# Two up tiles of a gated feed-forward from seven quarter products instead of eight

## The chip, the cores and the metric

The kernel runs on one core of one Trainium2 chip. The metric is the device time of one execution, in microseconds (us). The time of the kernel before is the median of three executions. Fractions of a microsecond per repetition matter here, because the part that is changed is repeated twenty times.

The engines are named as the profile names them: PE is the matrix engine, PEld its weight loads (they overlap PE), DVE the vector engine, ACT the scalar engine, POOL the general-purpose one, and SP the queue that issues the transfers (DMAs). Each engine works its own instructions in order, and engines wait for each other by semaphores.

## The reference, cut to what matters

The model is a two-layer decoder trunk on 512 tokens of width 1024. Only the feed-forward block of each layer matters for the change:

```python
def rms_norm(x, g):
    y = x * lax.rsqrt(jnp.mean(x * x, axis=-1, keepdims=True) + EPS)
    return y * g

def swiglu(h, w_gate_up, w_down):                  # D_FF = 2816 = 22 tiles of 128
    gu = h @ w_gate_up
    return (silu(gu[..., :D_FF]) * gu[..., D_FF:]) @ w_down

for layer in range(2):
    x = x + concat([mix_out, mem_o]) @ w_out[layer]
    x = x + swiglu(rms_norm(x, ln_ffn[layer]), w_gate_up[layer], w_down[layer])
return rms_norm(x, ln_final)
```

The norm is `x * gain * rstd`, where `rstd` is one number for each token. The kernel projects `x * gain` and multiplies by `rstd` afterwards. Each of the gate and the up half has 22 tiles of 128 rows.

## The kernel before, in words

**Layout.** Everything is kept transposed: features on the 128 partitions, the 512 tokens (T) along the row. The width of 1024 (D) is eight tiles of 128 (KD = 8). A weight tile is `[128, 1024]`: for one tile of 128 outputs, its eight blocks of 128x128 lie side by side, block k for input tile k.

**Precision.** Every operand of a projection is split into a rounded part and a rest, `hi` and `lo` (`split`, `weight`, `pair`). ACT writes `hi` (`copy`, L137), DVE writes `lo = src - hi` (`tt`, L150). `mm3` issues three matmuls (L143): hi by hi, hi by lo, lo by hi. One projection of 1024 by 512 tokens (`project`) is 8 blocks times 3 = 24 matmuls of 512 columns, accumulated in one PSUM bank.

**Weights.** `load` starts the transfer of a raw tile into one of two buffers `wraw` (512 KB each); `weight` splits it into `whi` and `wlo`, three buffers each, used in turn. So a new split can be written when the matmuls of the projection three before it have read theirs, and a new transfer can start when the `lo` of the tile two before it is done.

**Feed-forward (`ffn`).** Two halves of 11 tiles. For each tile f of a half: project gate (PSUM tag `pj`) and up (tag `g`); DVE multiplies the gate by `rstd` into `fg`; ACT applies silu; POOL multiplies `fg` by `rstd` again; DVE multiplies it with the up result into `fu`, and `fu` is split into the pair that the down projection reads. Then the down projection: for each of 8 output tiles 33 matmuls over 11 blocks, and DVE adds the sum to `x[m]`. In layer 0 the rotary tables (`rope_tables`, some 20 DVE instructions and two sines) are written beside the first gate tiles. In layer 1 the last two down tiles are done in two halves of 256 tokens, with the final norm behind each (`final`, `store`).

**Order.** The program is written as if sequential; a scheduler then puts the instructions of each engine in order and adds the semaphores. That order is fixed before the run. The `output` stage (w_out) lies ahead of each feed-forward; it produces `x[m]`, the pairs `h[m]`, and the sum of squares behind `rstd`.

Of the kernel before, what the change touches and what calls it, by code (L numbers as in the profile page):

```python
# [9 lines left out]
F32 = mybir.dt.float32  # L10
# [8 lines left out]
P = 128  # L19
# [66 lines left out]
class Builder:  # L86
# [52 lines left out]
    def square(self, out, in_):  # L139
        return self.nc.scalar.activation(out, in_, AF.Square).ins  # L140

    def mm(self, out, lhsT, rhs, start=True, stop=True):
        return self.nc.tensor.matmul(out, lhsT, rhs, start=start, stop=stop).ins  # L143

    def tr(self, out, in_):
        k = in_.shape[0]
# [29 lines left out]
        self.nc.sync.dma_start(raw, src)  # L176
        return raw

    def weight(self, src, eng=None, raw=None, parts=1, pool=None):

        raw = self.load(src) if raw is None else raw
        n = raw.shape[1]
        hi = self.t(pool or self.wpool, [P, D], F32R, "whi", 3)[:, :n]
        lo = self.t(pool or self.wpool, [P, D], F32R, "wlo", 3)[:, :n]
        for i in range(parts):
            s = slice(i * n // parts, (i + 1) * n // parts)
            self.split(raw[:, s], hi[:, s], lo[:, s], eng or self.weng)
        return hi, lo

    def mm3(self, ps, w, k, act, start, stop):  # L190

        (wh, wl), (ah, al) = w, act
        s = slice(k * P, (k + 1) * P)
        self.mm(ps, wh[:, s], ah, start, False)
        self.mm(ps, wh[:, s], al, False, False)
        self.mm(ps, wl[:, s], ah, False, stop)

    def project(self, src, acts, tag="pj", order=range(KD), w=None):
        w = self.weight(src) if w is None else w
# [26 lines left out]
    def build(self):  # L226
        tc, nc, a = self.tc, self.nc, self.a
        with ExitStack() as st:
            opened = lambda name, **kw: tc.tile_pool(name=name, bufs=1, reuse_waits="tile", **kw)
            pool = lambda name, **kw: st.enter_context(opened(name, **kw))  # L230
            cp = pool("const")
            self.wpool, self.apool = pool("w"), pool("acta")
            self.dpool = pool("scratch", space=DRAM)
            self.load_constants(cp)
            self.weng = nc.vector
            with opened("layer0", side="right") as self.mpool:
                with self.banks(pj=3, g=2, sc=3):
                    with opened("early", side="right") as ep:
                        self.mem_and_norm(ep)
                        self.gates(ep)  # L240
                    with opened("gdn", side="right") as gp:
                        mix = self.gdn(gp)
                    self.bpool, xp = pool("actb"), pool("x")
                    self.x = [self.t(xp, [P, T], F32, f"x{k}") for k in range(KD)]
                    for k in range(KD):
                        nc.sync.dma_start(self.x[k], a["xT"][:, k, :])
                    self.rstd, self.cosT, self.sinT = (self.t(xp, [P, T], F32, n) for n in ("rstd", "cosT", "sinT"))
                    h = self.output(xp, 0, mix, self.bpool)
                with opened("ffn0", side="right") as fp, self.banks(pj=4, g=4):
                    self.ffn(fp, xp, 0, h, self.apool, rope=True)  # L250
            with self.banks(pj=2, g=1, qk=1, pt=2, sc=1):
                with opened("swa", side="right") as sp:
                    mix = self.swa(sp)
                h = self.output(xp, 1, mix, self.apool)
            with opened("ffn1", side="right") as fp, self.banks(pj=4, g=4):
                self.ffn(fp, xp, 1, h, self.bpool)
# [570 lines left out]
        return h  # L827

    def ffn(self, fp, xp, layer, h, apool, rope=False):
        nc, a = self.nc, self.a  # L830
        acc = self.acc
        half = FT // 2
        for f0 in (0, half):
            acts = []
            for f in range(f0, f0 + half):
                pg = self.project(a["wgu"][layer, 2 * f], h, "pj")
                pu = self.project(a["wgu"][layer, 2 * f + 1], h, "g")
                if f == 0:
                    self.rstd_from(acc)
                    self.use(SILU_SIN)  # L840
                g = self.t(fp, [P, T], F32, "fg", 2)
                self.tt(nc.vector, g, pg, self.rstd, ALU.mult)
                self.fn(g, g, AF.Silu)
                self.tt(nc.gpsimd, g, g, self.rstd, ALU.mult)
                u = self.t(fp, [P, T], F32, "fu", 2)
                self.tt(nc.vector, u, pu, g, ALU.mult)
                hl = self.pair(apool) if f - f0 < KD else self.pair(fp, f"ac{f - f0}")
                self.split(u, *hl)
                acts.append(hl)
                if rope and f == 4:  # L850
                    self.rope_tables(fp)
            self.acc = None
            tail = KD - 2 if f0 and layer else KD
            down = lambda m, j, n, **kw: self.weight(a["wdn"][layer, m][:, (f0 + j) * P:(f0 + j + n) * P], **kw)
            for m in range(tail):
                ps = self.bank("pj")
                for j, n in ((0, 6), (6, 5)):
                    w = down(m, j, n)
                    for k in range(n):
                        self.mm3(ps, w, k, acts[j + k], j + k == 0, j + k == half - 1)  # L860
                self.tt(nc.vector, self.x[m], ps, self.x[m], ALU.add)
                if f0:
                    self.acc = self.accumulate(xp, self.acc, self.x[m], m)
        if tail < KD:

            parts = (slice(0, T // 2), slice(T // 2, T))
            w = {m: [down(m, j, n, pool=fp if m == KD - 1 else None) for j, n in ((0, 6), (6, 5))] for m in range(tail, KD)}
            outs = [self.t(fp, [P, KD, t.stop - t.start], F32, f"fin{t.start}") for t in parts]
            for o, t in zip(outs, parts):
                for k in range(tail):  # L870
                    self.copy(o[:, k, :], self.x[k][:, t], scale=self.gain(G_FIN, k))
            ends = []
            for t in parts:
                acc = self.acc[:, t]
                for m in range(tail, KD):
                    ps = self.bank("pj")[:, t]
                    for k in range(half):
                        self.mm3(ps, w[m][k // 6], k % 6, [x[:, t] for x in acts[k]], k == 0, k == half - 1)
                    x = self.x[m][:, t]
                    self.tt(nc.vector, x, ps, x, ALU.add)  # L880
                    sq = self.t(fp, [P, T], F32, "sql", 2)[:, t]
                    self.square(sq, x)
                    if m < KD - 1:
                        nxt = self.t(fp, [P, T], F32, "sqb", 2)[:, t]
                        self.tt(nc.vector, nxt, acc, sq, ALU.add)
                        acc = nxt
                ends.append(self.final(fp, (acc, sq), t))
            for (ps, r), o, t in zip(ends, outs, parts):
                self.store(ps, r, o, t, tail)

    def rstd_from(self, acc, t=slice(0, T)):
        self.use(LN_EXP)
# [15 lines left out]
    def rope_tables(self, pool):  # L908
# [1 line left out]
        nc, a = self.nc, self.a  # L910
        pi = self.t(pool, [P, T], I32, "rpi")
        nc.sync.dma_start(pi, a["positions"].partition_broadcast(P))
        r = self.t(pool, [P, T], F32, "rr")
        n = self.t(pool, [P, T], F32, "rn")
        nc.vector.tensor_copy(r, pi)
        self.ts(r, r, self.consts[:, C_INV:C_INV + 1], ALU.mult)
        magic = 1.5 * 2.0 ** 23
# [6 lines left out]
        sn = self.t(pool, [P, T], F32, "rsn")  # L924
        self.fn(sn, r, AF.Sin)
        self.ts(self.sinT, sn, self.consts[:, C_SIGN:C_SIGN + 1], ALU.mult)

# [87 lines left out]
    def final(self, fp, squares, t):  # L1015
# [5 lines left out]
        l, r = (self.t(fp, [P, T], F32, n, 2)[:, t] for n in ("fl", "fr"))  # L1021
# [5 lines left out]
    def store(self, ps, r, o, t, done):  # L1027

        nc = self.nc
        rows = self.a["out"].rearrange("(k p) t -> p k t", p=P)  # L1030
        wide = lambda f, k: f.unsqueeze(1).to_broadcast([P, k, t.stop - t.start])
        send = lambda a, b: nc.sync.dma_start(rows[:, a:b, t], o[:, a:b, :])
        self.tt(nc.gpsimd, o[:, 0:2, :], o[:, 0:2, :], wide(r, 2), ALU.mult)
        for k in range(2, done, 2):
            self.tt(nc.vector, o[:, k:k + 2, :], o[:, k:k + 2, :], wide(ps, 2), ALU.mult)
            send(k, k + 2)
        for k in range(done, KD):
            self.stt(o[:, k, :], self.x[k][:, t], self.gain(G_FIN, k), ps, ALU.mult, ALU.mult)
        send(done, KD)
        send(0, 2)  # L1040


def layout(i):
# [56 lines left out]
```

## Time and profile before

| what | value |
|---|---|
| time, median of 3 | 1200.42 us (1200.05 to 1201.89) |
| the profiled execution's own time | 1200.59 us, with a span of 1198.8 us in the profile |
| PE busy | 1178.0 us (98%), 6042 matmuls |
| PEld busy | 962.2 us (80%) |
| DVE busy | 620.2 us (52%), 1056 instructions |
| ACT busy | 507.0 us (42%), 938 instructions |
| POOL busy | 92.3 us (8%), 61 instructions |
| granted TensorE clock | 0.998 |

The span goes from the first to the last instruction; the time has 1.8 us more around it. Matmuls are pipelined: a row of the profile gives one matmul from its issue to its modelled end, so the sum of the rows is more than PE's time, and what one costs in a stream is the distance from one start to the next. The name `out<-in` beside an instruction gives the tiles that it writes and reads.

### The profile page before, as it was taken

The page shows a single profiled execution, that of the slowest core. Times are in us where ns is not written, and L with a number is a line of the kernel's source. Part 1 is how long each engine was busy: PE and PEld are TensorE (multiplying, and loading weights), DVE is VectorE, ACT ScalarE, POOL GpSimd, SP SyncE. Part 2 cuts the span into 40 slices and gives each one's busy share as a digit, 9 for nine tenths or more (in the row PEclk, how much of TensorE's full clock was granted, in tenths as well). Part 3 has the DMA queues.
Part 4 walks back from the last instruction along what each step waited for, and adds up shares of the span by engine and source line. Part 5 has one row for each costly group of instructions (what it writes and reads, how often), then busy time and mean ns, then how long its engine had stood idle before and what let it go on. Part 6 is the DMA issues. An engine that isn't in the chain of part 4 may idle for free.

```text
span 1198.8 us, 15416 instructions
## 1 busy us (share of the span) xinstructions
PE 1178.0 (98%) x6042; PEld 962.2 (80%) x6042; DVE 620.2 (52%) x1056; ACT 507.0 (42%) x938; POOL 92.3 (8%) x61
## 2 busy tenths in 40 slices
PE   7999999999999999999999999999999999999997
PEld 6888777877888888888888876788888888888886
DVE  6654977767754433334434767764434333434343
ACT  7578672466432322232333546773323222323342
POOL 0310000000011110011110000000111100111100
PEclk9999999999999999999999999999999999999999
DMA  7424352324333223333323320113232233232232
GB/s 298 138 91 127 98 127 83 117 75 170 100 93 92 97 79 96 113 104 93 97 76 97 131 79 28 54 52 108 88 106 88 81 93 126 88 106 88 77 96 92
DMA packets 51037, 121.08 MB, mean 101 GB/s; under 512 B 14300, under 2 KB 17012, under 8 KB 50964
## 3 DMA queue, kind: packets, MB, share of 16 engines
q1 hardware_dynamic: 50964, 120.10, 31.9%
q8 instruction: 47, 0.77, 0.3%
q14 instruction: 26, 0.21, 0.1%
HBM read 113.12 MB, written 6.96 MB: 100 GB/s over the span
## 4 chain that ended last, share of the span: by engine, by line
PE 91%; DVE 5%; ACT 2%; DMA 1%; issue 0%; SPq 0%; DVEq 0%; ACTq 0%
PE pj L143 59%; PE g L143 24%; PE sc L143 6%; PE pt L147 1%; DVE wlo L150 1%; PE g L147 1%; ACT sm L131 1%; DMA wraw<-in_wmk 1%; DVE btmp L150 1%; DVE big L150 0%; DVE sm L739 0%; DMA big<-basein 0%; PE qk L143 0%; DVE q L150 0%; ACT whi L137 0%
## 5 line engine op out<-in xcount | busy, mean ns | idle before, releaser
L137 ACT ACTIVATE whi<-wraw 128x1024 fp32r<-128x1024 f32 (+2 forms) x213 | 207.6, 976 | 555.9 <-PE pj L143 348.0
L143 PE MATMUL pj<-h,whi 128*128 128x512 f32 (+1 forms) x980 | 382.7, 391 | 0.2
L143 PE MATMUL pj<-l,whi 128*128 128x512 f32 (+1 forms) x980 | 381.4, 389 | 0.0
L143 PE MATMUL pj<-h,wlo 128*128 128x512 f32 (+1 forms) x980 | 381.1, 389 | 0.0
L150 DVE TENSOR_TENSOR wlo<-wraw,whi 128x1024 fp32r<-128x1024 f32 (+2 forms) x213 | 238.4, 1119 | 143.8 <-ACT whi L137 143.3
L143 PEld LDWEIGHTS pj<-h,whi 128*128 128x128 f32 x980 | 184.0, 188 | 39.8 <-issue 3.1
L143 PEld LDWEIGHTS pj<-l,whi 128*128 128x128 f32 x980 | 184.2, 188 | 38.3 <-issue 2.0
L143 PEld LDWEIGHTS pj<-h,wlo 128*128 128x128 f32 x980 | 184.3, 188 | 38.0 <-issue 1.9
L150 POOL TENSOR_TENSOR fg<-fg,rstd 128x512 f32<-128x512 f32 x44 | 75.5, 1716 | 985.4 <-ACT fg L131 985.4
L143 PE MATMUL g<-h,wlo 128*128 128x512 f32 x380 | 148.1, 390 | 0.0
L143 PE MATMUL g<-l,whi 128*128 128x512 f32 x380 | 148.0, 389 | 0.0
L143 PE MATMUL g<-h,whi 128*128 128x512 f32 x380 | 147.9, 389 | 0.0
L150 DVE TENSOR_TENSOR fu<-g,fg 128x512 f32<-128x512 f32 x44 | 30.4, 692 | 142.6 <-PE g L143 139.9
L150 DVE TENSOR_TENSOR fg<-pj,rstd 128x512 f32<-128x512 f32 x44 | 30.4, 691 | 110.7 <-PE pj L143 110.4
L143 PEld LDWEIGHTS g<-h,wlo 128*128 128x128 f32 x380 | 71.3, 188 | 15.0 <-issue 0.2
L143 PEld LDWEIGHTS g<-h,whi 128*128 128x128 f32 x380 | 71.4, 188 | 14.7
L143 PEld LDWEIGHTS g<-l,whi 128*128 128x128 f32 x380 | 71.3, 188 | 14.8
L150 DVE TENSOR_TENSOR x<-pj,x 128x512 f32<-128x512 f32 (+1 forms) x46 | 30.6, 668 | 70.4 <-PE pj L143 70.4
L131 ACT ACTIVATE fg<-fg 128x512 f32<-128x512 f32 x44 | 27.7, 629 | 1.5 <-DVE fg L150 1.5
L153 DVE SCALAR_TENSOR_TENSOR qv<-pj,gains,qv 128x511 f32<-128x511 f32 (+2 forms) x36 | 26.7, 743 | 1.1 <-ACT qv L137 0.8
L137 ACT ACTIVATE h<-x,gains 128x512 fp32r<-128x512 f32 x32 | 22.1, 712 | 5.7 <-DVE x L150 5.7
L140 ACT ACTIVATE sq<-x 128x512 f32<-128x512 f32 x38 | 23.4, 623 | 2.4 <-DVE sq L150 0.8
(305 smaller groups left out, 1203.5 us busy)
## 6 DMA issues: line engine op xcount, KB each, us to landing
wraw<-in_wgu SPq DMA_DIRECT2D x88, 512.0 KB, 3.5
wraw<-in_win SPq DMA_DIRECT2D x26, 512.0 KB, 3.6
wraw<-in_wdn SPq DMA_DIRECT2D x32, 384.0 KB, 3.1
wraw<-in_wdn SPq DMA_DIRECT2D x32, 320.0 KB, 2.8
wraw<-in_wout SPq DMA_DIRECT2D x16, 512.0 KB, 3.5
wraw<-in_wq SPq DMA_DIRECT2D x8, 512.0 KB, 3.5
x<-in_xT SPq DMA_DIRECT2D x4, 512.0 KB, 8.2
wraw<-in_wmv SPq DMA_DIRECT2D x4, 512.0 KB, 9.0
```

The source lines that it names most:

```text
L131: ins = self.nc.scalar.activation(out, in_, func, **kw).ins
L137: self.copied = self.nc.scalar.activation(out, in_, AF.Copy, **kw).ins
L140: return self.nc.scalar.activation(out, in_, AF.Square).ins
L143: return self.nc.tensor.matmul(out, lhsT, rhs, start=start, stop=stop).ins
L147: return self.nc.tensor.transpose(out, in_, self.ident[:k, :k]).ins
L150: return eng.tensor_tensor(out=out, in0=a, in1=b, op=op).ins
L153: self.nc.vector.scalar_tensor_tensor(out=out, in0=in0, scalar=scalar, in1=in1, op0=op0, op1=op1)
```

## The change

**Up tiles in pairs (`up_pair`).** The first up tile of each half stays as it was. The other ten go two at a time. Two up tiles are a product of a 2x2 matrix of weight quarters (rows: the two tiles; columns: input tiles 0 to 3 and 4 to 7) with a 2x2 matrix of token quarters (rows: input tiles; columns: tokens 0 to 255 and 256 to 511). Plainly that is eight quarter products; Winograd's form of Strassen's scheme takes seven, of sums of quarters. Each quarter product is 4 blocks times 3 = 12 matmuls of 256 columns. DVE forms four sums of weights (`s12`, `s34`) for each pair, and these are split like any weight. Four sums of tokens are formed once for each layer (`token_sums`, split tiles `T`). Three quarter results are copied from PSUM by ACT (`held`) before further products are accumulated on the same bank (`pa` three times more, `pc` once).

**The second factor `rstd`.** POOL's multiplication is gone; instead DVE multiplies each down result by `rstd` before it adds it to `x[m]` (`add`).

**Moves.** The rotary tables come after the first down tile of the first half. Buffers are shared or renamed to make room: the second raw up tile of a pair has one buffer of its own (`load(src[1], fp, 1)`), the final output is collected in the tiles `T`, and `ffn0` is opened after the first layer's pool is closed.

The diff, cut to its core:

```diff
+        def add(x, ps, t=slice(0, T)):
+            d = self.t(fp, [P, T], F32, "fu", 3)[:, t]
+            self.tt(nc.vector, d, ps, self.rstd[:, t], ALU.mult)
+            self.tt(nc.vector, x, d, x, ALU.add)
...
-            for f in range(f0, f0 + half):
-                pg = self.project(a["wgu"][layer, 2 * f], h, "pj")
-                pu = self.project(a["wgu"][layer, 2 * f + 1], h, "g")
...
-                self.tt(nc.gpsimd, g, g, self.rstd, ALU.mult)
...
+            for f in range(f0 + 1, f0 + half, 2):
+                g = []
+                for i in range(2):
+                    if f == 1:
+                        for _ in range(2 - i):
+                            sums.append(self.token_sums(fp, layer, len(sums), h))
+                    g.append(gate(f + i))
+                if f == 1:
+                    sums.append(self.token_sums(fp, layer, len(sums), h))
+                for u in self.up_pair(fp, [a["wgu"][layer, 2 * (f + i) + 1] for i in range(2)], sums, g):
+                    put(u)
...
-                self.tt(nc.vector, self.x[m], ps, self.x[m], ALU.add)
+                add(self.x[m], ps)
...
+                if rope and f0 == 0 and m == 0:
+                    self.rope_tables(fp)
...
+    def token_sums(self, fp, layer, j, h):
...
+        self.ts(c, x0[:, q:], g0, ALU.mult)
+        self.stt(t[0], x0[:, :q], g0, c, ALU.mult, ALU.subtract)
+        self.stt(t[1], x1[:, q:], g1, t[0], ALU.mult, ALU.add)
+        self.stt(t[2], x1[:, q:], g1, c, ALU.mult, ALU.subtract)
+        self.stt(t[3], x1[:, :q], g1, t[1], ALU.mult, ALU.subtract)
+        hl = self.weight(None, raw=raw, pool=fp, tags=("T", "T"), bufs=8)
...
+    def up_pair(self, fp, src, sums, g):
...
+        a1 = self.load(src[0])
+        a2 = self.load(src[1], fp, 1)
+        a11, a12, a21, a22 = a1[:, :T], a1[:, T:], a2[:, :T], a2[:, T:]
+        w0 = self.weight(None, raw=a1)
+        s12, s34 = (self.t(fp, [P, D], F32, "ws", 2) for _ in range(2))
+        self.stt(s12[:, :T], a21, -1.0, a22, ALU.mult, ALU.subtract)
+        self.stt(s12[:, T:], s12[:, :T], -1.0, a11, ALU.mult, ALU.subtract)
+        w1 = self.weight(None, raw=s12)
+        self.tt(nc.vector, s34[:, T:], a12, s12[:, T:], ALU.subtract)
+        self.tt(nc.vector, s34[:, :T], a11, a21, ALU.subtract)
+        w2 = self.weight(None, raw=s34)
+        w3 = self.weight(None, raw=a22)
+        pa, pb, pc = (self.bank("g")[:, :q] for _ in range(3))
+
+        def product(ps, w, i, b, first):
+
+            for j in range(4):
+                self.mm3(ps, w, 4 * i + j, sums[j][b], first and j == 0, j == 3, not first)
...
+        product(pa, w0, 0, "11", True)
+        p1 = held(pa)
+        product(pb, w0, 1, "21", True)
+        self.tt(nc.vector, u[0][:, :q], pb, p1, ALU.add)
+        product(pc, w1, 0, "t1", True)
+        p5 = held(pc)
+        product(pa, w1, 1, "t2", False)
+        u2 = held(pa)
+        product(pc, w2, 1, "22", False)
+        self.tt(nc.vector, u[0][:, q:], pc, u2, ALU.add)
+        self.tt(nc.vector, u[0], u[0], g[0], ALU.mult)
+        product(pa, w2, 0, "t3", False)
+        self.tt(nc.vector, u[1][:, q:], pa, p5, ALU.add)
+        self.tt(nc.vector, u[1][:, q:], u[1][:, q:], g[1][:, q:], ALU.mult)
+        product(pa, w3, 0, "t4", False)
+        self.tt(nc.vector, u[1][:, :q], pa, g[1][:, :q], ALU.mult)
```

The seven products are called below P1 (`"11"`), P2 (`"21"`), P3 (`"t1"`), P4 (`"t2"`), P5 (`"22"`), P6 (`"t3"`) and P7 (`"t4"`), in the order of the code. In the built program the scheduler puts seven matmuls of the next gate projection between P6 and P7.

More of the change, by code (lines that the diff above doesn't have):

```diff
@@ L140, in square, with mm @@
         return self.nc.scalar.activation(out, in_, AF.Square).ins
-    def mm(self, out, lhsT, rhs, start=True, stop=True):
-        return self.nc.tensor.matmul(out, lhsT, rhs, start=start, stop=stop).ins
+    def mm(self, out, lhsT, rhs, start=True, stop=True, more=False):
+        return self.nc.tensor.matmul(out, lhsT, rhs, start=start, stop=stop, skip_group_check=more).ins
     def tr(self, out, in_):
@@ L177, in load, with weight @@
         return raw
-    def weight(self, src, eng=None, raw=None, parts=1, pool=None):
+    def weight(self, src, eng=None, raw=None, parts=1, pool=None, tags=("whi", "wlo"), bufs=3):
         raw = self.load(src) if raw is None else raw
         n = raw.shape[1]
-        hi = self.t(pool or self.wpool, [P, D], F32R, "whi", 3)[:, :n]
-        lo = self.t(pool or self.wpool, [P, D], F32R, "wlo", 3)[:, :n]
+        hi = self.t(pool or self.wpool, [P, D], F32R, tags[0], bufs)[:, :n]
+        lo = self.t(pool or self.wpool, [P, D], F32R, tags[1], bufs)[:, :n]
         for i in range(parts):
@@ L188, in weight, with mm3 @@
         return hi, lo
-    def mm3(self, ps, w, k, act, start, stop):
+    def mm3(self, ps, w, k, act, start, stop, more=False):
         (wh, wl), (ah, al) = w, act
         s = slice(k * P, (k + 1) * P)
-        self.mm(ps, wh[:, s], ah, start, False)
-        self.mm(ps, wh[:, s], al, False, False)
-        self.mm(ps, wl[:, s], ah, False, stop)
+        self.mm(ps, wh[:, s], ah, start, False, more)
+        self.mm(ps, wh[:, s], al, False, False, more)
+        self.mm(ps, wl[:, s], ah, False, stop, more)
     def project(self, src, acts, tag="pj", order=range(KD), w=None):
@@ L248, in build @@
                     h = self.output(xp, 0, mix, self.bpool)
-                with opened("ffn0", side="right") as fp, self.banks(pj=4, g=4):
-                    self.ffn(fp, xp, 0, h, self.apool, rope=True)
+            with opened("ffn0", side="right") as fp, self.banks(pj=4, g=4):
+                self.ffn(fp, xp, 0, h, self.apool, rope=True)
             with self.banks(pj=2, g=1, qk=1, pt=2, sc=1):
@@ L832, in ffn @@
         half = FT // 2
-        for f0 in (0, half):
-            acts = []
-            for f in range(f0, f0 + half):
-                pg = self.project(a["wgu"][layer, 2 * f], h, "pj")
-                pu = self.project(a["wgu"][layer, 2 * f + 1], h, "g")
[L838 to L843, printed above, removed]
-                self.tt(nc.gpsimd, g, g, self.rstd, ALU.mult)
[L845 to L851, printed above, removed]
+        acts, sums = [], []
@@ new lines, in gate, with put @@
+        def gate(f):
+            ps = self.project(a["wgu"][layer, 2 * f], h, "pj")
+            if f == 0:
+                self.rstd_from(acc)
+                self.use(SILU_SIN)
+            g = self.t(fp, [P, T], F32, "fg", 2)
+            self.tt(nc.vector, g, ps, self.rstd, ALU.mult)
+            self.fn(g, g, AF.Silu)
+            return g
+        def put(u):
+            n = len(acts)
+            acts.append(self.pair(apool) if n < KD else self.pair(fp, f"ac{n}"))
+            self.split(u, *acts[-1])
@@ new lines, in add @@
+        def add(x, ps, t=slice(0, T)):
+            d = self.t(fp, [P, T], F32, "fu", 3)[:, t]
+            self.tt(nc.vector, d, ps, self.rstd[:, t], ALU.mult)
+            self.tt(nc.vector, x, d, x, ALU.add)
+        for f0 in (0, half):
+            acts.clear()
+            g = gate(f0)
+            u = self.t(fp, [P, T], F32, "fu", 3)
+            self.tt(nc.vector, u, self.project(a["wgu"][layer, 2 * f0 + 1], h, "g"), g, ALU.mult)
+            put(u)
[9 more added lines that the diff above has]
+                for u in self.up_pair(fp, [a["wgu"][layer, 2 * (f + i) + 1] for i in range(2)], sums, g):
+                    put(u)
@@ L860, in ffn @@
                         self.mm3(ps, w, k, acts[j + k], j + k == 0, j + k == half - 1)
-                self.tt(nc.vector, self.x[m], ps, self.x[m], ALU.add)
+                add(self.x[m], ps)
                 if f0:
                     self.acc = self.accumulate(xp, self.acc, self.x[m], m)
+                if rope and f0 == 0 and m == 0:
+                    self.rope_tables(fp)
         if tail < KD:
             parts = (slice(0, T // 2), slice(T // 2, T))
-            w = {m: [down(m, j, n, pool=fp if m == KD - 1 else None) for j, n in ((0, 6), (6, 5))] for m in range(tail, KD)}
-            outs = [self.t(fp, [P, KD, t.stop - t.start], F32, f"fin{t.start}") for t in parts]
+            own = dict(pool=fp, tags=("T", "T"), bufs=8)
+            w = {m: [down(m, j, n, **(own if m == KD - 1 else {})) for j, n in ((0, 6), (6, 5))] for m in range(tail, KD)}
+            outs = [[self.t(fp, [P, D], F32, "T", 8).rearrange("p (k t) -> p k t", k=4) for _ in range(2)] for t in parts]
             for o, t in zip(outs, parts):
                 for k in range(tail):
-                    self.copy(o[:, k, :], self.x[k][:, t], scale=self.gain(G_FIN, k))
+                    self.copy(o[k // 4][:, k % 4, :], self.x[k][:, t], scale=self.gain(G_FIN, k))
             ends = []
@@ L879, in ffn @@
                     x = self.x[m][:, t]
-                    self.tt(nc.vector, x, ps, x, ALU.add)
-                    sq = self.t(fp, [P, T], F32, "sql", 2)[:, t]
+                    add(x, ps, t)
+                    sq = self.t(fp, [P, T], F32, "fg", 2)[:, t]
                     self.square(sq, x)
                     if m < KD - 1:
-                        nxt = self.t(fp, [P, T], F32, "sqb", 2)[:, t]
+                        nxt = self.t(xp, [P, T], F32, "sqa", 2)[:, t]
                         self.tt(nc.vector, nxt, acc, sq, ALU.add)
@@ L889, in ffn @@
                 self.store(ps, r, o, t, tail)
+    def token_sums(self, fp, layer, j, h):
+        q = T // 2
+        g0, g1 = (self.gain(G_FFN[layer], j + i) for i in (0, 4))
+        x0, x1 = self.x[j], self.x[j + 4]
+        c = self.t(fp, [P, q], F32, "fc", 2)
+        raw = self.t(fp, [P, D], F32, "ws", 2)
+        t = [raw[:, i * q:(i + 1) * q] for i in range(4)]
+        self.ts(c, x0[:, q:], g0, ALU.mult)
[4 more added lines that the diff above has]
+        hl = self.weight(None, raw=raw, pool=fp, tags=("T", "T"), bufs=8)
+        parts = {f"t{i + 1}": [x[:, i * q:(i + 1) * q] for x in hl] for i in range(4)}
+        parts["11"] = [x[:, :q] for x in h[j]]
+        parts["21"], parts["22"] = ([x[:, i * q:(i + 1) * q] for x in h[j + 4]] for i in range(2))
+        return parts
@@ new lines, in up_pair, with held @@
+    def up_pair(self, fp, src, sums, g):
+        nc = self.nc
+        q = T // 2
+        a1 = self.load(src[0])
[14 more added lines that the diff above has]
+                self.mm3(ps, w, 4 * i + j, sums[j][b], first and j == 0, j == 3, not first)
+        def held(ps):
+            o = self.t(fp, [P, q], F32, "fs", 3)
+            self.copy(o, ps)
+            return o
+        u = [self.t(fp, [P, T], F32, "fu", 3) for _ in range(2)]
+        product(pa, w0, 0, "11", True)
[14 more added lines that the diff above has]
+        self.tt(nc.vector, u[1][:, :q], pa, g[1][:, :q], ALU.mult)
+        return u
@@ L912, in rope_tables @@
         nc.sync.dma_start(pi, a["positions"].partition_broadcast(P))
-        r = self.t(pool, [P, T], F32, "rr")
-        n = self.t(pool, [P, T], F32, "rn")
+        r = self.t(pool, [P, D], F32, "ws", 2)[:, :T]
+        n = self.t(pool, [P, T], F32, "fu", 3)
         nc.vector.tensor_copy(r, pi)
@@ L923, in rope_tables @@
         self.ts(r, r, math.pi * (1 - 1e-7), ALU.min, -math.pi * (1 - 1e-7), ALU.max)
-        sn = self.t(pool, [P, T], F32, "rsn")
+        sn = self.t(pool, [P, D], F32, "ws", 2)[:, :T]
         self.fn(sn, r, AF.Sin)
@@ L1020, in final @@
             self.mm(ps, self.ones, sq, k == 0, k == len(squares) - 1)
-        l, r = (self.t(fp, [P, T], F32, n, 2)[:, t] for n in ("fl", "fr"))
+        two = self.t(fp, [P, D], F32, "ws", 2)
+        l, r = (two[:, i * T:(i + 1) * T][:, t] for i in range(2))
         self.fn(l, ps, AF.Ln, scale=1.0 / D, bias=self.eps)
@@ L1030, in store @@
         rows = self.a["out"].rearrange("(k p) t -> p k t", p=P)
-        wide = lambda f, k: f.unsqueeze(1).to_broadcast([P, k, t.stop - t.start])
-        send = lambda a, b: nc.sync.dma_start(rows[:, a:b, t], o[:, a:b, :])
-        self.tt(nc.gpsimd, o[:, 0:2, :], o[:, 0:2, :], wide(r, 2), ALU.mult)
+        wide = lambda f: f.unsqueeze(1).to_broadcast([P, 2, t.stop - t.start])
+        two = lambda k: o[k // 4][:, k % 4:k % 4 + 2, :]
+        send = lambda k: nc.sync.dma_start(rows[:, k:k + 2, t], two(k))
+        self.tt(nc.gpsimd, two(0), two(0), wide(r), ALU.mult)
         for k in range(2, done, 2):
-            self.tt(nc.vector, o[:, k:k + 2, :], o[:, k:k + 2, :], wide(ps, 2), ALU.mult)
-            send(k, k + 2)
+            self.tt(nc.vector, two(k), two(k), wide(ps), ALU.mult)
+            send(k)
         for k in range(done, KD):
-            self.stt(o[:, k, :], self.x[k][:, t], self.gain(G_FIN, k), ps, ALU.mult, ALU.mult)
-        send(done, KD)
-        send(0, 2)
+            self.stt(o[k // 4][:, k % 4, :], self.x[k][:, t], self.gain(G_FIN, k), ps, ALU.mult, ALU.mult)
+        send(done)
+        send(0)
 def layout(i):
```

## The prediction

> **What bounds the kernel now.** I read the page first, then the chain of waits through the feed-forward, then a stretch of it by engine.
>
> ```profile
> span 1198.8 us, 15416 instructions
> ...
> PE 1178.0 (98%) x6042; PEld 962.2 (80%) x6042; DVE 620.2 (52%) x1056; ACT 507.0 (42%) x938; POOL 92.3 (8%) x61
> ...
> PE 91%; DVE 5%; ACT 2%; DMA 1%; issue 0%; SPq 0%; DVEq 0%; ACTq 0%
> ```
>
> PE is busy nearly always, and 91% of the chain that ended last is PE's own work. In the chain in order of time, the feed-forward is one block behind the other:
>
> ```profile
> 347.52 5.44 PE pj L143 x24
> 352.96 5.44 PE g L143 x24
> ```
>
> Start, duration, engine, tile, count. A projection is 24 matmuls of 512 columns in 5.44 us, with nothing between: 5.44 / 24 = 0.2267 us each. Two feed-forward tiles (two gates, two ups) are 96 matmuls or 21.76 us. The next view is the load of the engines in about as long a stretch; the columns are its length and then busy time (and instructions) of PE, PEld, DVE, ACT and POOL, and the granted clock.
>
> ```profile
> 352.00:374.00 22.00, 22.00 (x99) 18.22 (x98) 8.87 (x10) 6.41 (x8) 3.60 (x2) 1.00 0.31 99
> 434.00:500.00 66.00, 66.00 (x291) 54.25 (x290) 22.69 (x27) 14.93 (x18) 0.00 (x0) 1.00 0.35 106
> ```
>
> The first is up and gate, the second mostly down projection. PE has no gap, the clock is full, DVE is at 40% and 34%. So time in the feed-forward falls only if PE has less to do, and whatever makes PE wait comes on top one for one.
>
> **What the change takes off PE.** For a pair of up tiles: before 2 x 24 = 48 matmuls of 512 columns, now 7 x 12 = 84 of 256. Pairs: 5 in each half, 2 halves, 2 layers, so 20. A stream of 256-column matmuls stands in the trace, at the memory keys and values (chain in order of time, then the groups of 29 to 37.5 us by shape: they hold that shape only, 3 x 16 and 3 x 8):
>
> ```profile
> 28.97 8.64 PE sc L143 x72
> ...
> L143 PE MATMUL sc<-mh,whi 128*128 128x256 f32 x16 | 4.5, 283 | 0.0
> ...
> L143 PE MATMUL sc<-whi,mh 128*128 128x256 f32 x8 | 2.3, 283 | 0.0
> ...
> L143 PEld LDWEIGHTS g<-h,whi 128*128 128x128 f32 x380 | 71.4, 188 | 14.7
> ```
>
> 8.64 / 72 = 0.1200 us each. That is more than half of 0.2267: each matmul has a fixed part of 2 x 0.1200 - 0.2267 = 0.0133 us, and there are now more of them. A pair costs 84 x 0.1200 = 10.08 us in place of 48 x 0.2267 = 10.88. **The saving is 0.80 us for each pair, 20 x 0.80 = 16.0 us in all**, 7.4% of the ups instead of the eighth that the count of products promises. The weight load lasts 0.188 us by its row, more than 0.120; still the 72 follow each other every 0.120 us, each with its own load, so loads overlap.
> The Trainium skill (TensorE: Matmul & The Clock Gate, "Back-to-back issue gap") gives a warm gap of N / 2.4 + 2.5 ns; by it the pair would go from 10.36 to 9.17 us, and the whole saving would be an estimated 23.7 us. The trace's fixed part is 13.3 ns and not 2.5, and the sum goes by the trace.
>
> **What it adds beside PE.** The prices, by shape (busy, mean ns):
>
> ```profile
> L137 ACT ACTIVATE whi<-wraw 128x1024 fp32r<-128x1024 f32 x147 | 155.5, 1059 | 377.7 <-PE pj L143 221.2 <-PE g L143 141.0 <-issue 6.5
> L137 ACT ACTIVATE whi<-wraw 128x512 fp32r<-128x512 f32 x2 | 1.2, 614 | 0.0
> L137 ACT ACTIVATE pf<-pt 128x256 f32<-128x256 f32 x6 | 2.2, 373 | 1.1 <-PE pt L147 0.9
> L150 DVE TENSOR_TENSOR wlo<-wraw,whi 128x1024 fp32r<-128x1024 f32 x147 | 179.9, 1224 | 72.7 <-ACT whi L137 72.4
> L150 DVE TENSOR_TENSOR wlo<-wraw,whi 128x512 fp32r<-128x512 f32 x2 | 1.4, 691 | 0.1
> L153 DVE SCALAR_TENSOR_TENSOR rr<-rn,rr 128x512 f32<-128x512 f32 x10 | 6.9, 688 | 0.2
> L150 DVE TENSOR_TENSOR x<-pj,x 128x256 f32<-128x256 f32 x4 | 1.7, 425 | 6.4 <-PE pj L143 6.4
> L153 DVE SCALAR_TENSOR_TENSOR ml<-mem,gains,mh 128x256 fp32r<-128x256 f32 x8 | 3.5, 483 | 5.4 <-ACT mh L137 5.4
> ```
>
> DVE for each pair: the four weight sums 2 x 0.688 + 2 x 0.691 = 2.8; splits of three and a half tiles instead of two, 3 x 1.224 + 0.691 - 2 x 1.224 = 1.9; results in five pieces of 256 and one of 512 instead of two of 512, 5 x 0.425 + 0.691 - 2 x 0.691 = 1.4. That is 6.1 on top of 8.87, or 15 of the 21 us that a period then lasts. ACT: 6.41 + 1.06 + 0.61 + 3 x 0.37 = 9.2. Both have room as a total, so the question is the order within a period.
>
> **The order in a period.** I set t = 0 at the start of the second gate and run PE without a gap: gate to 5.44, P1 to 6.88, P2 8.32, P3 9.76, P4 11.20, P5 12.64, P6 14.08, seven matmuls of the next gate 15.67, P7 17.11, the rest of that gate 20.96. The steps that I need:
>
> ```profile
> 352.34 0.39 PE L143 MATMUL pj<-l,whi 128*128 128x512 f32 x1
> ...
> 352.82 1.06 ACT L137 ACTIVATE whi<-wraw 128x1024 fp32r<-128x1024 f32 x1 [3.83 <-PE pj L143]
> 353.79 0.63 ACT L131 ACTIVATE fg<-fg 128x512 f32<-128x512 f32 x1
> ...
> 332.70 0.68 DVE L150 TENSOR_TENSOR fg<-pj,rstd 128x512 f32<-128x512 f32 x1
> 333.30 1.21 DVE L150 TENSOR_TENSOR wlo<-wraw,whi 128x1024 fp32r<-128x1024 f32 x1
> 334.43 1.78 DVE L150 TENSOR_TENSOR rr<-rr,rn 128x512 f32<-128x512 f32 x1
> ...
> 12.30 1.24 DVE wlo L150
> ...
> 13.59 0.39 PE L143 MATMUL pj<-mh,wlo 128*128 128x256 f32 x1 [0.46 <-DVE wlo L150]
> 13.81 0.28 PE L143 MATMUL pj<-mh,whi 128*128 128x256 f32 x1
> ```
>
> A split's `hi` starts 0.48 us after the start of the last matmul that reads its buffer (352.34 to 352.82), so some 0.37 with 256 columns. ACT issues the next instruction 0.97 after a `hi` of 1024 columns; DVE goes on 0.60 after 512 columns, 1.13 after 1024, and by its 0.425 us some 0.34 after 256 (estimated). PE starts 0.05 after what it waited for (12.30 + 1.24 to 13.59), and the first step after a wait is 0.22 instead of 0.12: a wait costs 0.10 on top.
>
> - P4, P5, P6 and P7 write on banks that somebody has just read. P4 waits for ACT's copy of P1 (over before 8), P5 for that of P3 (started about 10.0, over at 10.3, due 11.20): no cost.
> - **P6 waits for ACT's copy of what P4 left.** On ACT, ahead of that copy, stands the `hi` of the next gate, which waits for P4 too, to get its buffer. `hi` starts at 10.96 + 0.37 = 11.33, the copy at 12.30, it ends at 12.68, PE goes on at 12.73. P6 was due at 12.64. Wait 0.09, restart 0.10: **0.19 us for each pair, 3.8 in all**. It could be 0 if the copy is a little faster than its row, or some 0.5 if ACT comes late.
> - P7 waits for DVE to read P6's sum. DVE's queue from 12.43: `lo` of the next gate to 13.56, right half of the first up to 13.90, first sum of the next pair to 14.56 (taken as 0.66), first up times gate to 15.16, then the read in question, over at 15.59. P7 is due at 15.67, and with P6's delay 15.86. No cost, but a margin of 0.1 to 0.3 only; bounds 0 and 0.4.
> - The `lo` of the next gate is due at 14.5 (third matmul) and done at 13.7; `hi` and `lo` of the others are done 3 us or more ahead.
>
> **The rest of the change.** The token sums are, for each layer, 16 instructions at up to 0.483, 4 shorter, and 4 `lo` at 1.224: at most 14.5 us of DVE, beside the end of `output` and the first gates:
>
> ```profile
> 275.00:319.00 44.00, 43.60 (x189) 34.99 (x188) 39.11 (x58) 21.98 (x31) 0.00 (x0) 1.00 0.44 146
> 796.00:840.00 44.00, 44.00 (x194) 36.06 (x193) 26.79 (x34) 20.75 (x28) 0.00 (x0) 1.00 0.34 108
> ```
>
> DVE is 39.11 of 44 us busy in layer 0 (with the rotary tables) and 26.79 in layer 1 (without), and PE is not held up in either. The change moves the tables (a difference of 12.3 us) into the down projection, where DVE has 43 of 66 us free, and puts the sums in their place. The sums are due only at P3, some 25 us after the first gate starts. I take 0; if the matmul for `rstd`, now right behind the first gate, waits for a late sum of squares, up to 1 us in each layer. POOL's multiplications go; they were off the path (PE had no gap). The second factor costs DVE 0.69 for each down tile of 33 x 0.2267 = 7.5 us, hidden by PE's next tile; only the last one has no cover:
>
> ```profile
> 1190.10 0.44 DVE x L150
> ...
> 1190.55 0.42 ACT sql L140
> ...
> 1191.02 0.71 PE g L143 x2
> ```
>
> The step at 1190.10 becomes two: 0.45 longer. The same chain for the first 256 tokens (0.92 by these rows, 0.3 ahead of it, now 1.65) has 1.4 us of matmuls as its cover: 0.3. Together 0.75.
>
> **Sum:** 16.0 - 3.8 - 0.75 = 11.4 us less. From the profiled execution, 1200.59 (span 1198.8 and 1.8 around it; the median is 1200.42, the same within 0.2): 1189.1 us.
>
> **Rivals.**
> 1. *All waits hidden.* P6's copy just makes it, the tail is covered: 1200.6 - 16.0 + 0.4 = 1185. For it: the computed wait is 0.09, less than my steps are sure of.
> 2. *More is lost in each pair, yet not all*: P6 0.3, P7 0.2, and 1 us at each layer's start: 16 - 10 - 2.75 = 3 us left, 1197.
> 3. *Slower: the single buffer of the second raw up tile.* Its transfer can start only when w3's `lo` is done (ACT 8.41 to 9.02, DVE to 9.74), and DVE's first sum of the next pair, which reads it, is queued ahead of the two instructions on which P7 waits.
>
> ```profile
> wraw<-in_wgu SPq DMA_DIRECT2D x88, 512.0 KB, 3.5
> ...
> x<-in_xT SPq DMA_DIRECT2D x8, 256.0 KB, 5.7
> ...
> rpi<-in_positions SPq DMA_DIRECT2D x1, 256.0 KB, 5.0
> ```
>
> With 3.5 us to landing it is there at 13.3, due at 13.90: 0.6 to spare, and 0.2 more ahead of P7. A landing time of 3.5 + 0.6 + 0.2 + 0.6 = 4.9 us eats the remaining 0.61 for each pair; above that the kernel is slower. The rows above with 5.0 and 5.7 are from crowded stretches; 5.7 is 0.8 beyond that point, or 20 x 0.8 = 16 us slower, with the tail 1217. Against it: the 88 tiles land in 3.5 at the median, with DMA at 0.31 of its share, and the change transfers no more.
> 4. *Weight loads set the pace of 256-column matmuls:* 84 x 0.188 = 15.8 us for a pair, 98 us slower, 1299. The 72 in 8.64 us, each with a load, speak against it. The Trainium skill (the same page, "What overlaps and what doesn't") says that a weight load overlaps with matmuls in flight only when their row groups differ, which here they don't; by that rule this rival would come true, and the trace disagrees (0.120 with loads of 0.188).
>
> **How the numbers follow.** Forecast (one short wait for each pair, 1186 to 1194): 0.55. Rival 1: 0.17. Rival 2: 0.14, of which 0.05 end within 0.2% (2.4 us, about what a measurement of this kernel can tell from no change). Rival 3: 0.11. Rival 4: 0.02; 0.01 that the change does not do what it says. Faster: 0.55 + 0.17 + 0.09 = 0.81; the same 0.05; slower 0.14. The range goes from rival 1 with the tail hidden too, 1184, to rival 2, 1197; outside are rivals 3 and 4 and the edge of 2.
>
> **What would show it.** Right: in the chain, quarter products of 12 in 1.44 us; a pair in 10.1 to 10.4; a wait of PE on ACT's `fs` of about 0.1, some 20 times, and nearly none on DVE `fu`; DVE near 15 us in 21; down blocks unchanged. Wrong: 256-column matmuls farther apart than 0.120; PE waits on `fu` or `whi` of half a microsecond in each pair; idle DVE ended by the transfer of `wraw`; a clock below 1.00.

## The result, and the profile after

The changed kernel takes **1188.97 us** (median; 1188.34 to 1191.16) against 1200.24 (1199.88 to 1201.89) for the kernel before, now the median of four executions: a ratio of 0.9907, 95% interval 0.989 to 0.9924. The profiled execution took 1188.53 us. The forecast was 1189.1 us.

The page of the changed kernel: span, then busy time by engine, then the chain that ended last by engine.

```profile
span 1186.8 us, 17191 instructions
...
PE 1164.9 (98%) x6762; PEld 982.7 (83%) x6762; DVE 766.6 (65%) x1338; ACT 566.7 (48%) x1046; POOL 16.8 (1%) x17
...
PE 92%; DVE 4%; ACT 2%; DMA 1%; issue 0%; SPq 0%; DVEq 0%; ACTq 0%
```

PE still sets the time. It has 720 matmuls more and is busy 13 us less; DVE has gained 146 us of work that the chain does not show. One period of a pair in the chain in order of time (start, duration, what, count):

```profile
336.17 8.77 PE g L143 x72
344.93 1.62 PE pj L143 x7
346.55 1.44 PE g L143 x12
347.99 9.34 PE pj L143 x41
357.33 8.77 PE g L143 x72
```

Six products, seven matmuls of the next gate, P7, the rest of that gate and the next: 357.33 - 336.17 = 21.16 us. Without a wait it would be 20.96, and before it was 21.76. P7 runs at its full pace (12 x 0.120 = 1.44); the six products take 8.77 in place of 8.64.

Where the 12.0 us of span went is read from three marks in the chain: in each layer the start of the fourth of the eight tiles of `output` (48 matmuls are the fourth and fifth of them; the first gate follows five tiles later), and the end of the last down matmul. `output` is the same in both kernels, so the marks compare like with like. First the kernel before, then the changed one.

```profile
286.56 10.97 PE pj L143 x48
...
800.03 10.88 PE pj L143 x48
...
1182.81 7.26 PE pj L143 x61
```

```profile
286.09 10.97 PE pj L143 x48
...
793.44 10.88 PE pj L143 x48
...
1170.75 6.79 PE pj L143 x57
```

| stretch | before | after | difference |
|---|---|---|---|
| up to the mark in `output` of layer 0 | 286.56 | 286.09 | -0.47, no part of the change (see the last section) |
| from there to the mark of layer 1 | 513.47 | 507.35 | -6.12 |
| from there to the end of the last down matmul | 390.04 | 384.10 | -5.94 |
| from there to the end of the span | 8.73 | 9.26 | +0.53 |

The two stretches that hold the twenty pairs bring 12.06 us, 0.60 for each pair, as the period does (21.76 - 21.16); the tail takes 0.53 back. The change is worth 11.5 us.

### The profile page after: what moved, and what is told of

Its sections match the earlier page's. It is cut to its first block, busy times and chain, and to the rows that moved or that the text cites. A ratio compares the mean times of both kernels' runs of the same rounds, so it can differ in the third digit from the quotient of the medians.

```text
span 1186.8 us, 17191 instructions
## 1 busy us (share of the span) xinstructions
PE 1164.9 (98%) x6762; PEld 982.7 (83%) x6762; DVE 766.6 (65%) x1338; ACT 566.7 (48%) x1046; POOL 16.8 (1%) x17
## 4 chain that ended last, share of the span: by engine, by line
PE 92%; DVE 4%; ACT 2%; DMA 1%; issue 0%; SPq 0%; DVEq 0%; ACTq 0%
PE pj L143 61%; PE g L143 23%; PE sc L143 6%; PE pt L147 1%; DVE wlo L150 1%; PE g L147 1%; ACT sm L131 1%; DMA wraw<-in_wmk 1%; ACT whi L137 0%; DVE sm L739 0%; PE qk L143 0%; DVE q L150 0%; DVE btmp L150 0%; DVE mx L743 0%; DVE big L150 0%
## 5 line engine op out<-in xcount | busy, mean ns | idle before, releaser
L143 PE MATMUL g<-T,whi 128*128 128x256 f32 x640 | 118.8, 285 | 0.2 <-ACT fs L137 0.2
L143 PEld LDWEIGHTS g<-T,whi 128*128 128x128 f32 x640 | 99.3, 189 | 4.7 <-DVE fu L150 1.1
L137 ACT ACTIVATE whi<-ws 128x1024 fp32r<-128x1024 f32 x40 | 42.4, 1060 | 117.5 <-PE pj L143 106.4
L143 PE MATMUL g<-h,whi 128*128 128x256 f32 (+1 forms) x300 | 92.0, 307 | 0.0
L143 PE MATMUL g<-h,wlo 128*128 128x256 f32 (+1 forms) x300 | 91.5, 305 | 0.0
L143 PE MATMUL g<-l,whi 128*128 128x256 f32 (+1 forms) x300 | 91.4, 305 | 0.0
L143 PE MATMUL g<-T,wlo 128*128 128x256 f32 x320 | 90.3, 282 | 0.0
L143 PEld LDWEIGHTS g<-T,wlo 128*128 128x128 f32 x320 | 60.3, 189 | 0.0
L150 DVE TENSOR_TENSOR fu<-pj,rstd 128x512 f32<-128x512 f32 (+1 forms) x34 | 22.4, 660 | 55.9 <-PE pj L143 55.9
L150 DVE TENSOR_TENSOR wlo<-ws,whi 128x1024 fp32r<-128x1024 f32 x40 | 49.0, 1224 | 6.7 <-ACT whi L137 6.3
```

Of the source, the lines that this page charges most:

```text
L137: self.copied = self.nc.scalar.activation(out, in_, AF.Copy, **kw).ins
L150: return eng.tensor_tensor(out=out, in0=a, in1=b, op=op).ins
```

## The experiments

All runs but the last four were timed beside a kernel before of 1202.07 us (1199.57 to 1202.99). The last four ran on another chip, beside a kernel before of 1201.12 (13 executions, 1199.59 to 1202.82), so between the two groups the ratios are compared. "First theory" in what was expected is the theory of the prediction.

**The changed kernel again**, as the ground for the others.

> The changed kernel itself, beside the kernel before on the same chip, as the measure for the three others. First theory (one short wait for each pair, of P6 on the copy after P4): 1189, ratio 0.990 to before; PE a period of 21.16 us in the chain.

1189.18 us (1188.06 to 1189.71), ratio 0.9896 (0.9878 to 0.9914), period 21.14.

**The copy after P4 on DVE.** The copy does not have to stand in ACT's queue:

```diff
-        u2 = held(pa)
+        u2 = held(pa, True)        # nc.vector.tensor_copy in place of ACT's copy
```

> The copy of what P4 leaves is made by DVE, which stands idle there, and no longer stands behind the next gate's hi on ACT. First theory: DVE copies from 11.4 to 11.8, P6 (due 12.64) does not wait, each period falls from 21.16 to 20.96 to 21.0 us, in all 3 to 4 us less than the changed kernel: 1185 to 1186. Rival: the 0.2 us over the ideal period are no wait but dearer matmuls after each change of width or bank; then the period stays at 21.16 and the time at 1189.

**1185.95 us** (1185.37 to 1186.76), ratio 0.9871 (0.9856 to 0.9886): 3.2 us less than the changed kernel. Its chain, and below it DVE's copy in order of time (start, duration, instruction, idle time before it and what ended that):

```profile
358.26 8.59 PE g L143 x72
366.85 1.62 PE pj L143 x7
368.47 1.42 PE g L143 x12
369.89 9.29 PE pj L143 x41
379.19 8.59 PE g L143 x72
```

```profile
364.02 0.42 DVE L960 COPY fs<-g 128x256 f32<-128x256 f32 x1 [1.56 <-PE g L143]
```

Six products in 8.59, a period of 379.19 - 358.26 = 20.93: the wait is gone. DVE had been idle for 1.56 us when P4 ended, so the copy starts at once.

**The copy ahead of the split, still on ACT.** This tells the queue from the engine:

```diff
+            if self.kept_copy is not None:                    # in weight(), next gate
+                self.nosync(self.copied, self.kept_copy)      # hi after the copy
```

> The copy stays on ACT but is ordered ahead of the next gate's hi. First theory: P6 does not wait (copy over at 11.8), but hi, lo and all of DVE's queue behind them come some 0.4 us later, and P7, now behind eight matmuls of the gate, waits 0 to 0.2 us on DVE: between the changed kernel and the one with the copy on DVE, 1185 to 1188. Rival (no wait, dearer matmuls): 1189.

1186.99 us (1186.43 to 1188.79), ratio 0.9881 (0.9865 to 0.9898). In its chain P6's wait is gone too:

```profile
356.83 8.59 PE g L144 x72
365.41 1.84 PE pj L144 x8
367.26 1.53 PE g L144 x12
368.79 9.10 PE pj L144 x40
```

P7 now takes 1.53 in place of 1.42: with the split later, DVE's steps behind it are later, and the rest of the gain turns into a wait of 0.1 for `fu`. So it was the place in the queue, and not ACT's speed.

**P7's cover taken away.** The seven matmuls of the next gate are ordered behind P7's first:

```diff
+        if self.behind is not None:
+            self.nosync(ins, self.behind)     # first matmul of the gate after P7
```

> The seven matmuls of the next gate between P6 and P7 are put behind P7, so P7 stands right behind P6 and waits for DVE to have read P6's sum. First theory, by the changed kernel's trace: P6's last matmul gives way at 365.93, DVE's read ends at 367.21; 1.33 us of wait and 0.10 for the restart in each of 20 pairs, 28.6 us more: 1217.6 (some of it less, if the wait lets DVE run ahead). Rival: the read is quick when nobody is in front of it, 0.7 us a pair: 1203.

1214.46 us (1213.63 to 1216.68), ratio 1.011 (1.0093 to 1.0128): slower than the kernel before. PE's waits (total, times, longest):

```profile
PE g L144 <- DVE fu L152: 21.1, 20, 1.2
```

21.1 us of waits and 20 restarts at 0.10 make 23.1 of the 25.3 us that it is above the changed kernel; the other 2 are not assigned. Expected were 28.6, with 1.33 of wait in every pair: in the trace it is 1.17 in most pairs, and in the last pair of each half only 0.52 to 0.87. The seven matmuls (1.6 us) are worth more than the whole change, and the scheduler put them there.

**Two buffers for the second raw up tile** (the third rival of the prediction):

```diff
-        a2 = self.load(src[1], fp, 1)
+        a2 = self.load(src[1], fp, 2)
```

> The changed kernel with two buffers in place of one for the second raw up tile of a pair, so that its transfer can start about a whole period earlier. The profiled changed kernel shows no DVE instruction that waits for that transfer. First theory (the transfer is hidden): the same time as the changed kernel, 1189 us, +-2; the wait on the copy after P4 stays at about 0.2 us for each pair. In this kernel P7 stands behind four matmuls of the next gate in place of seven, which may cost up to 0.3 us for each pair if DVE's read of P6's sum is then late (up to 6 us). Rival (the single buffer holds up DVE's sums and through them PE): at least 0.2 us less for each pair, 1185 us or below.

1189.81 us (1188.52 to 1190.33), ratio 0.9908 (0.9892 to 0.9925): the same as the changed kernel. The six products keep their 8.77; P7, with less cover, takes 1.46:

```profile
356.98 8.77 PE g L143 x72
365.75 0.93 PE pj L143 x4
366.68 1.46 PE g L143 x12
368.14 10.02 PE pj L143 x44
```

The trace of the changed kernel agrees. The first sum of each pair is the first to read the second raw tile (groups: busy, mean ns, idle before):

```profile
L153 DVE SCALAR_TENSOR_TENSOR ws<-wraw 128x512 f32<-128x512 f32 x20 | 13.7, 684 | 0.0
```

In 20 pairs DVE never waited ahead of it. The rival is out.

**The narrow matmul by itself.** The kernel before, with each up projection done as two halves of the tokens:

```diff
-                pu = self.project(a["wgu"][layer, 2 * f + 1], h, "g")
+                pu = self.halves(a["wgu"][layer, 2 * f + 1], h, "g")   # 2 x 24 matmuls of 256
```

> The kernel before with nothing of the change but the narrower matmul: every up projection is done as two halves of 256 columns, 48 matmuls of 256 in place of 24 of 512, the same products in all. It measures the price of the narrow matmul by itself. First theory (each matmul has a fixed part of 13.3 ns): 44 projections x (48 x 0.1200 - 5.44 us) = 44 x 0.32 = 14.1 us more than before, about 1214.5 us, ratio 1.012; the chain shows 48 matmuls in 5.76 us. Rival (fixed part of 2.5 ns, an estimate from the gap that the Trainium skill states in TensorE: Matmul & The Clock Gate, Back-to-back issue gap): 44 x 24 x 2.5 ns = 2.6 us more, 1203 us. Rival (the weight load of 0.188 us sets the pace of narrow matmuls): 44 x (48 x 0.188 - 5.44) = 158 us more, 1358 us.

1215.65 us (1214.83 to 1217.61), ratio 1.0124 (1.0109 to 1.014): 14.5 us more than before by the medians, 14.9 by the ratio.

```profile
350.60 5.47 PE pj L143 x24
356.07 5.75 PE g L143 x48
```

44 x (5.47 + 5.75 - 10.88) = 15.0 us. The fixed part of 13.3 ns accounts for 14.1 of it. The Trainium skill (TensorE: Matmul & The Clock Gate, "Back-to-back issue gap") gives 2.5 ns for the gap of an isolated matmul, and says itself that at small widths this formula leaves out the weight loads of a real stream; the prediction and the expectation left that condition out. With 2.5 ns the time would have been an estimated 1203 us, and this stream, with a load for every matmul, does not follow it. (The prediction's 23.7 us from the same formula is 20 x 1.19 = 23.8.) Nor does the load of 0.188 us set the pace: 5.75 / 48 = 0.120 us. So seven products for eight save 7.4% and not 12.5%, as the prediction had it.

**The second factor by itself.** The kernel before, without POOL's multiplication and with `rstd` on the down results:

```diff
-                self.tt(nc.gpsimd, g, g, self.rstd, ALU.mult)
...
-                self.tt(nc.vector, self.x[m], ps, self.x[m], ALU.add)
+                add(self.x[m], ps)
```

> The kernel before with the second part of the change alone: POOL's multiplication of the gate by rstd is gone, and DVE multiplies each down result by rstd before it adds it to x. First theory (hidden everywhere but behind the last two down tiles): 0.5 to 0.75 us more at the end of the span, 1201 us, the same within what can be told; between the last matmul of the down projections and the end of the span the profile shows 9.2 to 9.3 us in place of 8.7. Rival (POOL's work held something up, or slowed DVE): 1 us or more less than before. Rival (DVE's second instruction holds up PE at the down tiles): over 2 us more.

1201.63 us (1200.56 to 1203.74), ratio 1.0006 (0.9997 to 1.0015): in the time it can't be told from no change, as expected. The chain has it:

```profile
1183.84 6.78 PE pj L143 x57
...
1190.65 0.44 DVE fu L150
...
1191.11 0.44 DVE x L150
```

From the end of the last matmul, 1190.62, to the end of the span, 1199.8, are 9.18 us, 0.45 more than before. PE's waits show nothing new at the other down tiles.

**Both mended:** the copy on DVE, and the second factor back on POOL.

```diff
+            self.tt(nc.gpsimd, g, g, self.rstd, ALU.mult)
...
-        u2 = held(pa)
+        u2 = held(pa, True)
```

> The changed kernel with the copy after P4 on DVE (the run with that edit alone took 1185.95 us) and with the second factor put back on POOL, as in the kernel before: it takes the tail term out and keeps the seven products. First theory (the tail costs 0.5 us, and the products are bound by PE alone): 1185.4 us, +-1, with 8.7 us in place of 9.3 between the last down matmul and the end of the span. Rival (POOL's multiplication, 1.8 us for each gate, comes too late for DVE's product of the up result, or slows DVE): P7 waits for DVE, 0.2 us or more for each pair, 1189 us or more.

1186.15 us (1184.85 to 1188.01), ratio 0.9878 (0.9863 to 0.9892). By the time it is the same as the copy on DVE alone. In its chain:

```profile
289.15 10.97 PE pj L143 x48
...
1170.16 7.26 PE pj L143 x61
...
1177.45 0.43 DVE x L150
```

The tail is 1186.2 - 1177.42 = 8.78 us, back where it was before; but the mark in `output` of layer 0 is at 289.15, and at 287.22 in the run with the copy alone. Counted from there, this one takes 897.05 us and that one 897.28: of the expected 0.5 the one pair of profiles shows 0.2, which is too little to be sure of. POOL's multiplication held nothing up.

## Why the prediction was right, point by point

**The saving on PE: predicted 0.80 for each pair.** It stands: with the copy on DVE the period is 20.93 (20.96 predicted, 21.76 before). From the first mark to the end of the span that kernel is 14.96 us below the kernel before (897.28 against 912.24); with 0.5 for the tail put back that is 15.5 of the 16.0. The run with both mended, where the tail is as before, gives 912.24 - 897.05 = 15.2. Beside PE, one period (336.17 to 357.33) has 13.99 us of DVE (predicted 15, as the sum of rows; neighbouring rows of one engine overlap by some 0.08) and 9.09 of ACT (9.2).

**P6's wait: predicted 0.09 and 0.10 for the restart.** PE, ACT and DVE of the changed kernel in order of time:

```profile
364.20 0.28 PE L143 MATMUL g<-h,wlo 128*128 128x256 f32 x1
364.40 0.51 PE L143 MATMUL g<-T,whi 128*128 128x256 f32 x2
364.74 0.28 PE L143 MATMUL g<-T,wlo 128*128 128x256 f32 x1
...
367.55 0.40 PE L143 MATMUL g<-T,whi 128*128 128x256 f32 x2
```

```profile
363.02 1.06 ACT L137 ACTIVATE whi<-wraw 128x1024 fp32r<-128x1024 f32 x1 [0.97 <-PE g L143]
363.98 0.37 ACT L137 ACTIVATE fs<-g 128x256 f32<-128x256 f32 x1
```

```profile
364.11 1.23 DVE L150 TENSOR_TENSOR wlo<-wraw,whi 128x1024 fp32r<-128x1024 f32 x1 [2.58 <-ACT whi L137]
365.25 0.42 DVE L150 TENSOR_TENSOR fu<-g,fs 128x256 f32<-128x256 f32 x1
365.58 0.68 DVE L153 SCALAR_TENSOR_TENSOR ws<-wraw 128x512 f32<-128x512 f32 x1
366.18 0.69 DVE L150 TENSOR_TENSOR fu<-fu,fg 128x512 f32<-128x512 f32 x1
366.79 0.42 DVE L150 TENSOR_TENSOR fu<-g,fs 128x256 f32<-128x256 f32 x1
```

P5's last matmul, at 364.20, stands at 12.52 on the prediction's scale, so its zero is at 351.68:

| step | predicted | measured |
|---|---|---|
| `hi` of the next gate starts | 11.33 | 11.34 |
| copy after P4, start and end | 12.30, 12.68 | 12.30, 12.67 |
| P6 goes on (due 12.64) | 12.73 | 12.72 |
| DVE: `lo`, right half, first sum, up times gate | 12.43, 13.56, 13.90, 14.56 | 12.43, 13.57, 13.90, 14.50 |
| DVE has read P6's sum | 15.59 | 15.53 |
| P7 starts | 15.86 | 15.87 |

P6 is 0.08 late, and its first two matmuls take 0.34 in place of 0.24. The price is 0.18 by the rows of six products (8.77 against 8.59) and 0.23 by the period (21.16 against 20.93); predicted were 0.19. The last pair of a half shows the cause without an experiment. There the `hi` ahead of the copy belongs to a down tile and has 768 columns:

```profile
603.54 0.84 ACT L137 ACTIVATE whi<-wraw 128x768 fp32r<-128x768 f32 x1 [0.97 <-PE g L143]
604.29 0.37 ACT L137 ACTIVATE fs<-g 128x256 f32<-128x256 f32 x1
```

The copy starts 0.75 after that `hi` and not 0.97, and the six products of that pair take 8.59: no wait.

So the step was right, but not its count. The prediction charged the wait to all twenty pairs, 3.8 us; the last pair of each of the four halves has none, and the first pair of layer 1 pays more, since its `hi` comes 0.27 later than in the others (why is not shown):

```profile
850.63 0.50 PE L143 MATMUL g<-T,whi 128*128 128x256 f32 x2 [0.19 <-ACT fs L137]
```

This is the only wait for `fs` that the list of PE's waits has; the others, of 0.08, are read from the starts. The six products of that pair take 9.03. The rows of six products make 15 x 0.18 + 0.44 = 3.1 us in all, and the copy on DVE gained 3.2 by the times and 900.71 - 897.28 = 3.4 from the first mark on.

**P7: predicted no cost, a margin of 0.1 to 0.3.** The margin is 15.87 - 15.53 - 0.05 = 0.29, and it is spent in the runs that shorten its cover: 0.1 over where the split comes 0.3 us later, 1.2 where the cover is gone. The edge was as near as it was said to be. For four of the twenty pairs the premise does not hold: in the last pair of a half no gate follows, and only three or four down matmuls stand between P6 and P7, not seven. P7 then takes 1.51 to 1.63 in place of 1.44, 0.4 us in all that the prediction put at nothing:

```profile
606.43 0.70 PE pj L143 x3
607.13 1.51 PE g L143 x12
```

**Token sums: predicted 0, up to 1 us a layer.** The stretches by engine, of the end of `output` and the first gates of each layer (length, busy time of PE, PEld, DVE, ACT and POOL, then clock):

```profile
285.00:330.00 45.00, 45.00 (x197) 36.74 (x196) 37.68 (x58) 25.10 (x33) 0.00 (x0) 1.00 0.41 136
795.00:837.00 42.00, 42.00 (x185) 34.42 (x184) 38.27 (x58) 22.72 (x29) 0.00 (x0) 1.00 0.37 117
```

PE without a gap at a full clock, DVE at up to 38 of 42 us. Right: P1 to P4 of the first pair run without a gap in both layers (48 matmuls in 5.74 us in layer 1), so the sums were there at P3. In the prediction's own row for layer 0, PE is busy 43.60 of 44.00 us, so "not held up" is not quite so: the 0.40 is one wait for DVE at 275.73, in a part that the change leaves alone.

**Tail: predicted 0.75, measured 0.53.** The 0.45 at the end came as predicted (0.45 in the run with that edit alone). The 0.3 in the middle did not: between the two sums of squares of the first 256 tokens stand nine down matmuls in place of five, and the cover was long enough. Before, then changed:

```profile
1181.58 0.59 PE pj L143 x5
...
1169.22 1.06 PE pj L143 x9
```

**The rivals.** The first (all waits hidden, 1185) is what one line on another engine makes of this kernel, 1185.95. The second needed 0.5 of waits for each pair, and the pairs have 0.2. The third fell with the run with two buffers and the row without idle time, the fourth by 0.120 us for each narrow matmul. That the sum of 11.4 us meets 11.5 so closely is in part luck, because three errors cancel: the saving is 0.5 short (15.5 of 16.0, mostly P7 in the last pairs), the waits of P6 cost 0.4 less (3.4 in place of 3.8), and the tail 0.2 less (0.53 in place of 0.75). The profiled execution has 0.5 us of chance from the part ahead of the first mark besides.

## What to carry to other kernels

Price a product that is cut in pieces by the distance of matmuls of the very width that it will have: here half the width costs 0.53 of the time, and that takes 5 of the 12.5% that seven for eight promises. Where one engine is never idle, write the queue of every other engine out for one period, in order and with issue steps: what matters is not the load of ACT (9 us of 21) but that a copy of 0.37 us, which PE waits for, stands behind a split of 1 us, which nobody needs yet. Then move that copy to the engine that is idle at that instant.

## What the runs showed of the hardware that was not expected

- Changes of width have a price of their own. In the run with halves, 24 matmuls of 512 columns behind a narrow stretch take 5.47 us in place of 5.44. In the changed kernel the narrow six take 8.59 where 72 x 0.120 = 8.64, and seven wide ones 1.62 where 7 x 0.2267 = 1.59: the two nearly cancel.
- The part ahead of the first mark, at which none of these edits aims, ended between 285.69 and 289.15 us in ten profiles. Those 3.5 us are as much as P6's wait costs in all, so that for small edits the distances between marks in the chain told more than the times. What makes that part vary is not shown.
